# Recurrence gates of a hybrid encoder layer on TensorE: two heads in the two row halves, both gates in the columns

## The chip, the cores and the metric

The kernel runs on one core of one Trainium2 chip. The metric is the device time of one execution in microseconds (us); lower is better. The engines are TensorE (PE, whose weight loads are listed apart as PEld), VectorE (DVE), ScalarE (ACT), GpSimd (POOL) and SyncE (SP), which here only asks for transfers. A line number such as L821 is a line of the kernel before.

## The reference, cut to what matters

One layer on 512 tokens of width 1024: a half-step SwiGLU FFN, a mixer with two branches (a gated linear recurrence, and sliding-window attention), and a second half-step FFN. The change is in the recurrence's gates, which are block-diagonal: 16 heads of 64 channels, each with its own 64x64 matrix for each of two gates.

```python
def rg_lru(x, wa, ba, wx, bx, lam):
    xb = xf.reshape(b, s, LRU_BLOCKS, LRU_BLOCK)          # 16 heads of 64 channels
    r = jax.nn.sigmoid(jnp.einsum('bshi,hij->bshj', xb, wa).reshape(b, s, LRU_WIDTH) + ba)
    ig = jax.nn.sigmoid(jnp.einsum('bshi,hij->bshj', xb, wx).reshape(b, s, LRU_WIDTH) + bx)
    log_a = -LRU_C * r * jax.nn.softplus(-lam)
    a = jnp.exp(log_a)
    u = jnp.sqrt(-jnp.expm1(2.0 * log_a)) * (ig * xf)
    # then the scan h[t] = a[t] * h[t-1] + u[t] over the tokens
```

x here is the input projection's x_rnn after a causal convolution of four taps.

## The kernel before

**Precision.** A float32 product is made of three matmuls in the fp32r format: each operand is split into a high part (ACT copies it) and a rest (DVE subtracts), and high x high, rest x high and high x rest are added up in one PSUM bank. `split2` (L188) splits activations, `split_to` (L148) the weights: L155 on ACT, L156 on DVE.

**Layout.** Activations are kept channels x tokens: a tile is 128 channels by 512 tokens, one PSUM bank (`bank`, 8 of them). A "unit" (`unit`, L206) is one 128-channel tile of a projection: `mm_feat` (L193) makes 24 matmuls of 512 columns (lines L200 to L202). Weights come in 512 KB pieces by transfers that SP asks for in a fixed `order` (L99), as buffers come free. All big tiles come from one pool of 42 buffers (`slot`), in turn.

**Order of work.** PE's order is that of the program text. What ACT, DVE and POOL do beside a unit is put in by `later(n, fn, rank)` (L174): it is due n points later, and `point()` (L178), called twice in a unit, runs what is due. So the order on every engine is fixed when the program is built, and each engine works its own list in order, waiting on semaphores.

**The recurrence.** After the first FFN the eight x_rnn tiles are made (`xr`), then the first eight of the branch gates (`wg`), then k, v, q. Beside them, for each of the eight channel tiles i: `conv`; `rg_gates(i)` (L810) splits the convolved tile into `xs`, and two points later `products` (L818) puts six matmuls of 128 rows x 128 columns x 512 tokens between the units' matmuls, three for each gate, into the banks `r` and `i`. The weight of a gate is a 128x128 block with the two heads' 64x64 matrices on its diagonal and zeros elsewhere; `rg_load` (L780) clears a buffer on POOL, brings the matrices in with two transfers and splits it, once for each gate. One point later `gates` (L825) takes a tanh of each bank on ACT (L826, L827) and one product on DVE (L828); a sigmoid is made from the tanh of half its argument, so the biases are halved once in `softplus` (L704). `rg_decay` and `rg_scan` follow.

**The start.** Nine matmuls on zeros (L602) warm PE. Then ACT's list has a table load with a one-column square root (L607) and the request for the first 128 rows of x transposed (`load_x(0, act)`, L608); SP asks for the vector of small parameters (`vec`, L609), for the weights of the first three units in quarters (`load_w`) and for the other rows of x. L642, L643 and L649 to L651 are the split of x and the first units' matmuls.

Of the kernel before, what the change touches and what calls it, by code (L numbers as in the profile page):

```python
# [10 lines left out]
F32 = mybir.dt.float32  # L11
F32R = mybir.dt.float32r
AF = mybir.ActivationFunctionType
ALU = mybir.AluOpType

P = 128
SEQ = 512
D = 1024
KT = D // P
# [12 lines left out]
V_CW, V_CB, V_BA, V_BX, V_LAM, V_BG, V_G1, V_SINK, V_N = 0, 32, 40, 48, 56, 64, 80, 88, 104  # L32
# [19 lines left out]
def hybrid_layer(ctx: ExitStack, tc: tile.TileContext, a: dict, out: bass.AP):  # L52
    nc = tc.nc
    act, dve, pool, pe, sp = nc.scalar, nc.vector, nc.gpsimd, nc.tensor, nc.sync

    cp = ctx.enter_context(tc.tile_pool(name="cp", bufs=1))
# [6 lines left out]
    def slot(shape, dt=F32, name="s"):  # L63
        uid[0] += 1
        return sb.tile(shape, dt, tag="slot", name=f"{name}_{uid[0]}")

    def bank(name="ps"):
        uid[0] += 1
        return pp.tile([P, 512], F32, tag="ps", name=f"{name}_{uid[0]}")

    def small(w, name="m", bufs=4):
        uid[0] += 1
        return sm.tile([P, w], F32, tag=f"sm{w}", name=f"{name}_{uid[0]}", bufs={1: 11, 4: 12}.get(w, bufs))

    def f32(ap):
        return ap.bitcast(F32)
# [3 lines left out]
    vec = cp.tile([P, V_N], F32, name="vec")  # L80
    chalf = cp.tile([P, KT], F32, name="chalf")
    cneg = cp.tile([P, KT], F32, name="cneg")
    bhalf = cp.tile([P, 4 * KT + 8], F32, name="bhalf")

    cp.tile([P, 192], F32, name="gap")
    sm.tile([P, 256], F32, name="gap2", bufs=1)
    uT = cp.tile([P, 2, KT, SEQ], F32R, name="uT")

# [71 lines left out]
    def get(nm, i, ahead=2, rawahead=3):  # L160

        k = st["get"]
        assert order[k] == (nm, i), (order[k], nm, i)
        dma_to(k + 1 + ahead)
        split_to(k + 1 + ahead)
        dma_to(st["split"] + rawahead)
        st["get"] += 1
        return pairs.pop(k)
# [5 lines left out]
    def later(n, fn, rank=1):  # L174
        uid[0] += 1
        due.append((now[0] + n, rank, uid[0], fn))
# [11 lines left out]
    def split2(hi, lo, src):  # L188

        act.activation(hi, src, AF.Copy)  # L190
        dve.tensor_tensor(out=lo, in0=src, in1=f32(hi), op=ALU.subtract)  # L191
# [14 lines left out]
    def unit(nm, i, **kw):  # L206
        w = get(nm, i)
        ps = bank("f")
        mm_feat(ps, w, **kw)
        return ps  # L210
# [12 lines left out]
    def rstd_of(ssq, scale=1.0, during=lambda q: None):  # L223

        n = ssq.shape[-1]
        w = 1 if n == 2 else n
        v, q, r, e, r2 = (small(w, x) for x in ("v", "q", "r", "e", "r2"))
        if n == 2:
            dve.tensor_scalar(out=v, in0=ssq[:, 0:1], scalar1=ssq[:, 1:2], scalar2=D * EPS, op0=ALU.add, op1=ALU.add)
        else:  # L230
            dve.tensor_scalar(out=v, in0=ssq, scalar1=D * EPS, scalar2=None, op0=ALU.add)
        act.activation(q, v, AF.Sqrt)
        during(q)
        dve.reciprocal(r, q)
        if w == 1:
            dve.scalar_tensor_tensor(out=e, in0=r, scalar=v, in1=r, op0=ALU.mult, op1=ALU.mult)
        else:
            dve.tensor_tensor(out=e, in0=r, in1=r, op=ALU.mult)
            dve.tensor_tensor(out=e, in0=e, in1=v, op=ALU.mult)
        s = scale * D**0.5  # L240
        dve.tensor_scalar(out=e, in0=e, scalar1=-0.5 * s, scalar2=1.5 * s, op0=ALU.mult, op1=ALU.add)
        dve.tensor_tensor(out=r2, in0=r, in1=e, op=ALU.mult)
        return r2
# [160 lines left out]
    def silu_mul(ps1, ps3, R=None):  # L404

        t = slot([P, 2, SEQ], name="sw")
        if R is None:
            act.activation(t[:, 0, :], ps1, AF.Silu)
            dve.tensor_tensor(out=t[:, 1, :], in0=ps3, in1=t[:, 0, :], op=ALU.mult)
        else:  # L410
            dve.tensor_tensor(out=t[:, 0, :], in0=ps1, in1=R, op=ALU.mult)
            dve.tensor_tensor(out=t[:, 1, :], in0=ps3, in1=R, op=ALU.mult)
            act.activation(t[:, 0, :], t[:, 0, :], AF.Silu)
            dve.tensor_tensor(out=t[:, 1, :], in0=t[:, 1, :], in1=t[:, 0, :], op=ALU.mult)
        return t[:, 1, :]
# [173 lines left out]
    def load_x(k, q=sp):  # L589
        q.dma_start(out=xts[k // 2][:, k % 2, :], in_=a["xT"][k * P : (k + 1) * P, :])  # L590
# [10 lines left out]
    for _ in range(WARM):  # L601
        pe.matmul(psw, warm[:, :P], warm, start=True, stop=True)  # L602


    tiny = small(4, "tiny")
    dve.memset(tiny, 1.0)
    act.activation(tiny, tiny, AF.Sqrt)  # L607
    load_x(0, act)  # L608
    sp.dma_start(out=vec, in_=a["vec"])  # L609
    for kp in range(KT // 2):  # L610
        load_w(0, kp)
# [18 lines left out]
    ps = [bank("f") for _ in range(NS)]  # L630
# [28 lines left out]
    r = rstd_of(s4, during=lambda q: act.activation(tiny, q, AF.Silu))  # L659
# [26 lines left out]
    def softplus():  # L686
# [16 lines left out]
        dve.tensor_scalar(out=cneg, in0=z[3], scalar1=-4.0, scalar2=None, op0=ALU.mult)  # L703
        dve.tensor_scalar(out=bhalf, in0=vec[:, V_BA : V_BG + 16], scalar1=0.5, scalar2=None, op0=ALU.mult)  # L704

    def swiglu_units(na, nb, f0, f1, hid, R=None):
        for f in range(f0, f1):
            p1, p3 = unit(na, f), unit(nb, f)
            later(1, lambda p1=p1, p3=p3: hid.f.append(silu_mul(p1, p3, R)))
# [45 lines left out]
    for i, at_ in enumerate((end - 5, end - 2, end - 1)):  # L755
        later(at_, lambda i=i: pairs_a.prep(1, i))
    swiglu_units("w1a", "w3a", 2, NC1, hid, Rb)
    point(True)
    X1["b21"] = to_uT(xn[1, 0], 1, 0)
# [17 lines left out]
    hid = None  # L777


    def rg_load(nm):  # L780
        r = slot([P, KT, P], name="rgraw")
        pool.memset(r, 0.0)
        v = a[nm].rearrange("(i two) p q -> two p i q", two=2)
        pool.dma_start(out=r[0:64, :, 0:64], in_=v[0])
        pool.dma_start(out=r[64:128, :, 64:128], in_=v[1])
        hi = slot([P, KT, P], F32R, name="rghi")
        lo = slot([P, KT, P], F32R, name="rglo")
        act.activation(hi, r, AF.Copy)
        dve.tensor_tensor(out=lo, in0=r, in1=f32(hi), op=ALU.subtract)
        return hi, lo  # L790

    rga, rgx = rg_load("rg_a_w"), rg_load("rg_x_w")

    def vcol(base, i):
        return vec[:, base + i : base + i + 1]

    def hcol(base, i):
        return bhalf[:, base - V_BA + i : base - V_BA + i + 1]
# [11 lines left out]
    def rg_gates(i):  # L810
        s0 = lru[i]
        s1 = slot([P, 2, SEQ], name="ig_e")
        lru[i] = (s0, s1)
        xs = slot([P, 2, SEQ], F32R, name="xcs")
        xc, t, ig = s0[:, 0, :], s0[:, 1, :], s1[:, 0, :]
        split2(xs[:, 0, :], xs[:, 1, :], xc)

        def products():  # L818
            pr, pi = bank("r"), bank("i")
            for ps, (wh, wl) in ((pr, rga), (pi, rgx)):  # L820
                pe.matmul(ps, wh[:, i, :], xs[:, 0, :], start=True, stop=False)  # L821
                pe.matmul(ps, wh[:, i, :], xs[:, 1, :], start=False, stop=False)
                pe.matmul(ps, wl[:, i, :], xs[:, 0, :], start=False, stop=True)

            def gates():  # L825
                act.activation(t, pr, AF.Tanh, scale=0.5, bias=hcol(V_BA, i))  # L826
                act.activation(ig, pi, AF.Tanh, scale=0.5, bias=hcol(V_BX, i))  # L827
                dve.scalar_tensor_tensor(out=ig, in0=ig, scalar=1.0, in1=xc, op0=ALU.add, op1=ALU.mult)  # L828

            later(1, gates, 2)  # L830

        later(RG_LAG, products)
# [50 lines left out]
    for i in range(8):  # L883
        ps = unit("wg", i)
# [16 lines left out]
    for i in range(2):  # L901
        ps = unit("wk", i)
# [8 lines left out]
    for t in range(NT):  # L911
        ps = bank("v")
        c = slice(t * P, (t + 1) * P)
        o = ps[:, :256]
        for k in range(KT):
            wh, wl = wv[k // 4]
# [18 lines left out]
    for i in range(2):  # L935
        ps = unit("wq", i)
# [12 lines left out]
    for i in range(8):  # L949
        ps = unit("xg", i)  # L950
# [121 lines left out]
    for nm, i in att_units:  # L1072
        if nm == "lru":
            w = get(nm, i) if i else w_lru
            ps = bank("f")
# [5 lines left out]
        ps = unit(nm, i)  # L1081
# [4 lines left out]
    w = get("wao", 0)  # L1086
# [14 lines left out]
    for i in range(8):  # L1101
        if i:
            w = get("wao", i)
        ps = bank("f")
# [18 lines left out]
    for i, at_ in enumerate((end - 7, end - 4, end - 3, end - 2, end - 1)):  # L1123
        later(at_, lambda i=i: pairs_b.prep(0, i))
    later(end, lambda: pairs_b.prep(1, 0))
    swiglu_units("w1b", "w3b", 2, NC2, hid)
    point(True)
    X2["t4"] = to_uT(tn[3], 0, 1)
# [75 lines left out]
```

## Time and profile before

| | |
|---|---|
| time, median of 3 runs | 1140.14 us (1140.09 to 1140.4) |
| the profiled execution's own time | 1140.29 us |
| its span, first to last instruction | 1138.5 us |
| granted TensorE clock, mean | 0.999 |
| PE, DVE, ACT, POOL busy | 1129.9, 778.5, 572.0, 341.8 us |
| gate matmuls (bank r and bank i) | 48, first 405.8 us, last 460.0 us |

All times of the profile count from the start of the span. A matmul's listed duration is longer than the time from one start to the next, since matmuls are pipelined; so matmuls are priced by the distance of their starts. "Idle before" gives how long the engine sat idle ahead of an instruction, and what released it.

### The profile page before, as it was taken

The numbers are of one execution on the slowest core, as the hardware profiler recorded it, in microseconds if no ns is written. First come the engines' busy times: TensorE is split into PE (matmuls) and PEld (weight loads), VectorE is DVE, ScalarE is ACT, GpSimd is POOL, SyncE is SP. The second block draws the span as 40 slices with busy tenths as digits, with TensorE's granted clock in tenths as the row PEclk, the third lists the DMA queues.
The fourth block names the chain that finished last, engine by engine and source line by source line (L and its number), as shares of the span: only waits on it lengthen the run. The fifth ranks groups of instructions, "written<-read, shape, count | busy, mean of one in ns | idle before, by whom it ended". The sixth has DMA issues, their size and how long they took to land.

```text
span 1138.5 us, 17073 instructions
## 1 busy us (share of the span) xinstructions
PE 1129.9 (99%) x6691; PEld 1006.8 (88%) x6691; DVE 778.5 (68%) x1180; ACT 572.0 (50%) x1021; POOL 341.8 (30%) x259
## 2 busy tenths in 40 slices
PE   9999999999999999999999999999999999999997
PEld 7889999988889888888888888889899999998886
DVE  5997889885447746684678864667968678985313
ACT  7445555564325357844656662356445555574211
POOL 0148677500001000001555640000655567700000
PEclk9999999999999999999999999999999999999999
DMA  9943323265314311234122333532133332255101
GB/s 339 155 138 112 100 88 111 87 210 166 98 57 152 120 56 56 90 97 130 56 78 90 93 99 105 170 126 93 37 94 112 112 98 89 93 189 180 39 19 55
DMA packets 36800, 124.93 MB, mean 110 GB/s; under 512 B 4400, under 2 KB 5936, under 8 KB 36720
## 3 DMA queue, kind: packets, MB, share of 16 engines
q1 hardware_dynamic: 34128, 115.15, 30.6%
q0 software_dynamic: 2448, 8.43, 3.9%
q8 instruction: 52, 0.85, 0.3%
q10 hardware_dynamic: 144, 0.26, 0.1%
q14 instruction: 28, 0.23, 0.1%
HBM read 116.50 MB, written 7.33 MB: 109 GB/s over the span
## 4 chain that ended last, share of the span: by engine, by line
PE 94%; DMA 4%; DVE 1%; SPq 0%; ACT 0%; issue 0%; DVEq 0%; ACTq 0%
PE f L201 11%; PE f L202 11%; PE f L200 11%; PE c L453 10%; PE c L452 10%; PE c L451 10%; PE acc L219 8%; PE acc L218 8%; PE acc L220 8%; DMA raw_w1a<-in_w1a_dram 2%; PE pt L1019 1%; DMA h<-in_x_dram 1%; PE s L983 1%; PE s L982 1%; PE tr L291 1%; PE o L1035 1%
## 5 line engine op out<-in xcount | busy, mean ns | idle before, releaser
L200 PE MATMUL f<-uT,whi 128*128 128x512 f32 (+1 forms) x536 | 196.1, 366 | 0.0
L201 PE MATMUL f<-uT,wlo 128*128 128x512 f32 (+1 forms) x536 | 195.2, 364 | 0.3 <-DVE wlo L156 0.3
L202 PE MATMUL f<-uT,whi 128*128 128x512 f32 (+1 forms) x536 | 195.1, 364 | 0.0
L218 PE MATMUL acc<-whi,hT 128*128 128x512 f32 x352 | 137.1, 390 | 0.0
L219 PE MATMUL acc<-wlo,hT 128*128 128x512 f32 x352 | 137.0, 389 | 0.0
L220 PE MATMUL acc<-whi,hT 128*128 128x512 f32 x352 | 136.9, 389 | 0.0
L201 PEld LDWEIGHTS f<-uT,wlo 128*128 128x128 f32 x536 | 101.2, 189 | 16.4 <-DVE wlo L156 0.7
L191 DVE TENSOR_TENSOR wlo<-S,whi 128x1024 fp32r<-128x1024 f32 x68 | 112.8, 1659 | 4.1 <-ACT whi L190 3.8
L453 PE MATMUL c<-Xl,whi 128*128 128x256 f32 x408 | 115.5, 283 | 0.0
L453 PE MATMUL c<-uT,whi 128*128 128x256 f32 x408 | 115.5, 283 | 0.0
L452 PE MATMUL c<-Xh,wlo 128*128 128x256 f32 x408 | 115.5, 283 | 0.0
L452 PE MATMUL c<-uT,wlo 128*128 128x256 f32 x408 | 115.5, 283 | 0.0
L451 PE MATMUL c<-Xh,whi 128*128 128x256 f32 x408 | 115.5, 283 | 0.0
L451 PE MATMUL c<-uT,whi 128*128 128x256 f32 x408 | 115.5, 283 | 0.0
L202 PEld LDWEIGHTS f<-uT,whi 128*128 128x128 f32 x536 | 101.1, 189 | 15.9
L200 PEld LDWEIGHTS f<-uT,whi 128*128 128x128 f32 x536 | 101.2, 189 | 15.6
L1003 POOL TENSOR_SCALAR P<-P,d 128x256 f32<-128x256 f32 (+1 forms) x64 | 63.1, 1001 | 56.0 <-DVE d L1001 33.9
L452 PEld LDWEIGHTS c<-Xh,wlo 128*128 128x128 f32 x408 | 78.3, 192 | 0.0
L452 PEld LDWEIGHTS c<-uT,wlo 128*128 128x128 f32 x408 | 78.3, 192 | 0.0
L451 PEld LDWEIGHTS c<-Xh,whi 128*128 128x128 f32 x408 | 78.3, 192 | 0.0
L451 PEld LDWEIGHTS c<-uT,whi 128*128 128x128 f32 x408 | 78.3, 192 | 0.0
L453 PEld LDWEIGHTS c<-uT,whi 128*128 128x128 f32 x408 | 78.3, 192 | 0.0
(313 smaller groups left out, 2673.7 us busy)
## 6 DMA issues: line engine op xcount, KB each, us to landing
raw_w2a<-in_w2a_dram SPq DMA_DIRECT2D x22, 512.0 KB, 4.1
raw_w1b<-in_w1b_dram SPq DMA_DIRECT2D x22, 512.0 KB, 3.9
raw_w3b<-in_w3b_dram SPq DMA_DIRECT2D x22, 512.0 KB, 3.9
raw_w2b<-in_w2b_dram SPq DMA_DIRECT2D x22, 512.0 KB, 4.2
raw_w3a<-in_w3a_dram SPq DMA_DIRECT2D x21, 512.0 KB, 4.4
raw_w1a<-in_w1a_dram SPq DMA_DIRECT2D x20, 512.0 KB, 4.3
raw_wg<-in_wg_dram SPq DMA_DIRECT2D x16, 512.0 KB, 4.0
raw_xr<-in_xr_dram SPq DMA_DIRECT2D x8, 512.0 KB, 3.9
```

What stands on the lines that cost most here:

```text
L191: dve.tensor_tensor(out=lo, in0=src, in1=f32(hi), op=ALU.subtract)
L200: pe.matmul(ps[:, c0:c1], wh[:, s], h_, start=k == 0, stop=False)
L201: pe.matmul(ps[:, c0:c1], wl[:, s], h_, start=False, stop=False)
L202: pe.matmul(ps[:, c0:c1], wh[:, s], l_, start=False, stop=k == KT - 1)
L218: pe.matmul(acc[n], x[:, 0, c], wh[:, s], start=first, stop=False)
L219: pe.matmul(acc[n], x[:, 0, c], wl[:, s], start=False, stop=False)
L220: pe.matmul(acc[n], x[:, 1, c], wh[:, s], start=False, stop=last)
L291: pe.transpose(ps[:, k * P : (k + 1) * P], hg[:, kk * P : (kk + 1) * P], ident)
L451: pe.matmul(ps, wh[:, s], xh, start=first, stop=False, skip_group_check=True)
L452: pe.matmul(ps, wl[:, s], xh, start=False, stop=False, skip_group_check=True)
L453: pe.matmul(ps, wh[:, s], xl, start=False, stop=k == 3, skip_group_check=True)
L1003: pool.tensor_scalar(out=pt[:, x, b0:256], in0=pt[:, x, b0:256], scalar1=d[:, x : x + 1], scalar2=None, op0=ALU.mult)
```

## The change

A gate's two heads no longer share a 128-row matmul in which half of the weights are zero. One weight tile `rgw` holds both gates: in rows 0 to 63 (the lower head of the channel tile) columns 0 to 63 are the matrix of gate r and columns 64 to 127 that of gate i; in rows 64 to 127 (the upper head) it is the other way round. A matmul takes 64 rows of weights and of activations and gives both gates of one head. There are still six matmuls for a channel tile, now 64 rows x 128 columns x 512 tokens, in turn for rows 0 to 63 (bank `r`) and rows 64 to 127 (bank `i`). The tanh is taken in four pieces of 64 partitions, two of which go to the other half of the partitions, so `bxh` holds the halved bias of gate i in both halves (16 columns, taken off the unused `gap`). `rg_load` runs once, without a clear. Apart from that, the request for the first rows of x comes ahead of the square root on ACT's list.

```diff
-    cp.tile([P, 192], F32, name="gap")
+    bxh = cp.tile([P, 2, KT], F32, name="bxh")
+    cp.tile([P, 176], F32, name="gap")
...
+    load_x(0, act)
     tiny = small(4, "tiny")
     dve.memset(tiny, 1.0)
     act.activation(tiny, tiny, AF.Sqrt)
-    load_x(0, act)
     sp.dma_start(out=vec, in_=a["vec"])
...
         dve.tensor_scalar(out=bhalf, in0=vec[:, V_BA : V_BG + 16], scalar1=0.5, scalar2=None, op0=ALU.mult)
+        for par in range(2):
+            for r0 in (0, 64):
+                dve.tensor_scalar(
+                    out=bxh[r0 : r0 + 64, par, :], in0=vec[64 * par : 64 * par + 64, V_BX : V_BX + KT],
+                    scalar1=0.5, scalar2=None, op0=ALU.mult)
...
-    def rg_load(nm):
+    def rg_load():
         r = slot([P, KT, P], name="rgraw")
-        pool.memset(r, 0.0)
-        v = a[nm].rearrange("(i two) p q -> two p i q", two=2)
-        pool.dma_start(out=r[0:64, :, 0:64], in_=v[0])
-        pool.dma_start(out=r[64:128, :, 64:128], in_=v[1])
+        for nm, cs in (("rg_a_w", (0, 64)), ("rg_x_w", (64, 0))):
+            v = a[nm].rearrange("(i two) p q -> two p i q", two=2)
+            for par, c in enumerate(cs):
+                pool.dma_start(out=r[64 * par : 64 * par + 64, :, c : c + 64], in_=v[par])
...
-    rga, rgx = rg_load("rg_a_w"), rg_load("rg_x_w")
+    rgw = rg_load()
...
         def products():
-            pr, pi = bank("r"), bank("i")
-            for ps, (wh, wl) in ((pr, rga), (pi, rgx)):
-                pe.matmul(ps, wh[:, i, :], xs[:, 0, :], start=True, stop=False)
-                pe.matmul(ps, wh[:, i, :], xs[:, 1, :], start=False, stop=False)
-                pe.matmul(ps, wl[:, i, :], xs[:, 0, :], start=False, stop=True)
+            ps = bank("r"), bank("i")
+            for n, (w, x) in enumerate(((0, 0), (1, 0), (0, 1))):
+                for p_, r_ in zip(ps, (slice(0, 64), slice(64, P))):
+                    pe.matmul(p_, rgw[w][r_, i, :], xs[r_, x, :], start=n == 0, stop=n == 2)
 
             def gates():
-                act.activation(t, pr, AF.Tanh, scale=0.5, bias=hcol(V_BA, i))
-                act.activation(ig, pi, AF.Tanh, scale=0.5, bias=hcol(V_BX, i))
+                lo_, up = slice(0, 64), slice(64, P)
+                for p_, r_ in zip(ps, (lo_, up)):
+                    act.activation(t[r_], p_[r_], AF.Tanh, scale=0.5, bias=hcol(V_BA, i)[r_])
+                for par, (p_, r_, o_) in enumerate(((ps[0], up, lo_), (ps[1], lo_, up))):
+                    act.activation(ig[o_], p_[r_], AF.Tanh, scale=0.5, bias=bxh[r_, par, i : i + 1])
                 dve.scalar_tensor_tensor(out=ig, in0=ig, scalar=1.0, in1=xc, op0=ALU.add, op1=ALU.mult)
```

## The prediction, made before the changed kernel ran

> **What bounds the kernel.** I read the page's busy table first, then PE's waits, the timeline around one set of gate products, and the timelines of ACT beside it and of the start.
>
> ```profile
> PE 1129.9 (99%) x6691; PEld 1006.8 (88%) x6691; DVE 778.5 (68%) x1180; ACT 572.0 (50%) x1021; POOL 341.8 (30%) x259
> ```
>
> ```profile
> PE w L602 <- DVE tiny L606: 1.4, 1, 1.4
> PE f L201 <- DVE wlo L156: 0.3, 1, 0.3
> ```
>
> The first line is the share of the span, the others are all that PE waited for, in us, times and longest. Apart from its first 1.4 us PE stops once, for 0.3 us. So from about 1.5 us to the end the time is the sum of the distances between matmul starts, and what is taken off PE is taken off the end, until another engine or a transfer takes PE's place. The timeline of one channel tile (start, duration):
>
> ```profile
> 405.59 0.39 PE L202 MATMUL f<-uT,whi 128*128 128x512 f32 x1
> 405.81 0.39 PE L821 MATMUL r<-xcs,rghi 128*128 128x512 f32 x1
> ...
> 406.50 0.39 PE L821 MATMUL i<-xcs,rghi 128*128 128x512 f32 x1
> ...
> 407.18 0.39 PE L200 MATMUL f<-uT,whi 128*128 128x512 f32 x1
> ```
>
> Six gate matmuls and two of their neighbours: seven steps from 405.59 to 407.18 are 1.59 us, 0.227 us each. One tile's six cost 6 x 0.227 = 1.36 us, the eight tiles 10.9 us, all on the path.
>
> **The gate products.** The change keeps 48 matmuls of 512 columns, in 24 pairs whose halves use different rows of the array. No row shows two matmuls side by side, so a pair is bounded. Below, one step, 0.227 us. Above, two steps, 0.454 us, if the halves take turns; beyond that only if weight loads stop running ahead (a rival). I take 0.23: a pair also needs two weight loads of 128 columns, and the eight 128-column transposes L291 take 0.87 us, 0.109 us for a load and its matmul, so two loads (0.218 us) fit into a step.
>
> Between 128-row and 64-row matmuls the array changes its shape, once in and once out for a tile. The nearest rows are the only matmul of less than 128 rows (L667, 32 rows), and the restart after PE's only stop:
>
> ```profile
> 27.61 0.39 PE L202 MATMUL f<-uT,whi 128*128 128x512 f32 x1
> ...
> 27.93 0.11 PEld L667 LDWEIGHTS e<-oh 32*16 32x16 f32 x2 [0.35 <-issue]
> ...
> 28.26 0.48 PE L667 MATMUL e<-oh 32*16 32x384 f32 x1
> ...
> 28.67 0.19 PEld L676 LDWEIGHTS r<-dgs,ones 128*128 128x128 f32 x1 [0.64 <-issue]
> 28.67 0.38 PE L676 MATMUL r<-dgs,ones 128*128 128x128 f32 x1
> ...
> 57.56 0.19 PEld L201 LDWEIGHTS f<-uT,wlo 128*128 128x128 f32 x1 [0.70 <-DVE wlo L156]
> 57.56 0.50 PE L201 MATMUL f<-uT,wlo 128*128 128x512 f32 x1 [0.27 <-DVE wlo L156]
> ...
> 57.90 0.40 PE L202 MATMUL f<-uT,whi 128*128 128x512 f32 x1
> ```
>
> Into L667 the distance is 0.32 us instead of 0.227, 0.09 more; its weight load (PEld) begins with the matmul, not ahead of it. Out of it, 28.26 to 28.67 is 0.41 us against 0.33 from its first pass (27.93) to its second, 0.08 more. L667 loads only 16 columns. At 57.56 a 128-column load stood in the open, and the next start came 0.34 us later, 0.11 above a step. So I take 0.11 in and 0.08 out, 0.19 us for a tile. Below nothing it can't go; above, I take each change as waiting out the matmul before it (0.39 listed less the 0.227 step, 0.16) and then an open load (0.11), 0.54 us for the two.
>
> A tile then takes 3 x 0.23 + 0.19 = 0.88 us instead of 1.36, 0.48 saved, 8 x 0.48 = **3.84 us**. The ends are 8 x (0.68 - 0) = 5.4 and 8 x (0.68 - 0.54) = 1.1 us.
>
> The Trainium skill (TensorEngine Tiling, Key Properties) speaks against the change at this point: changing the tiling mode drains TensorE. The 0.09 and 0.08 us above agree that a change costs something, but not with a full wait for the matmul before (0.16).
>
> **The gates on ACT.** Two tanh of 128x512 (0.69 us each) become four of 64x512. Half the partitions are hardly cheaper: copies of 64x512 from PSUM (L892) take 0.59 us. So a tile adds 1.2 to 1.4 us to ACT. One turn of ACT, from one tile's gates to the next:
>
> ```profile
> 446.13 0.69 ACT L826 ACTIVATE xc_t<-r,bhalf 128x512 f32<-128x512 f32 x1 [1.15 <-PE r L823]
> 446.81 0.69 ACT L827 ACTIVATE ig_e<-i,bhalf 128x512 f32<-128x512 f32 x1
> ...
> 449.53 0.69 ACT L881 ACTIVATE g<-f,bhalf 128x512 f32<-128x512 f32 x1 [0.56 <-PE f L202]
> ...
> 450.96 0.82 ACT L840 ACTIVATE xc_t<-xc_t,chalf 128x512 f32<-128x512 f32 x1
> 452.93 0.69 ACT L826 ACTIVATE xc_t<-r,bhalf 128x512 f32<-128x512 f32 x1 [1.15 <-PE r L823]
> ```
>
> The turn is 6.80 us, and ACT idles 0.56 + 1.15 = 1.71 us in it, both times for PE. PE's turn becomes 6.80 - 0.48 = 6.32 us; ACT's work becomes 5.09 + 1.3 = 6.4. ACT is full and slips at most 0.2 us a turn, some 1.2 us over the six turns at this rate. What is late next: the products of DVE (L828) and behind them on its list the weight rests L156, whose wait for ACT grows by two tanh; and the weight copies L155 behind the tanh on ACT. PE takes these weights later: the rests for wq 0 are written by 472.8 us and first used at about 480; the tightest, for xg 2, by 497.86, used at about 502, and DVE is 98% busy from 480 to 500. That run begins behind ACT's square roots at 477.5; ACT idles 1.08 + 0.75 + 0.75 us between 463 and 476, which takes up the slip. Cover: 4 us of lead, of which 1 to 2 go. Cost nothing; if the cover were gone, the slip, 1.2 us. Bank r is now held through the third tanh, 1.3 us longer; a turn takes three of the eight banks, so a bank comes round after 2.7 turns, 17 us.
>
> **The small edits.** The single `rg_load` drops two POOL clears (0.96 us each), one ACT copy (1.06) and one DVE subtraction (1.22); its four transfers stay, on the same POOL queue. PE has no idle time from 360 to 380 us, so nothing is gained. The four `bxh` products of 64x8 go after L704 at 250.5 us, by the 128x8 rows near it 0.2 us each, 0.8 us on DVE, which is 93% busy from 245 to 255; behind them stand the rests of the second FFN matrix. DVE idles 0.73 us at 257 and 2.1 at 261, waiting, and PE never stops there: nothing, or 0.8 if the cover failed. Three buffers fewer shift later tiles in the pool and so the waits of SP's weight transfers; those are asked for far ahead (wk at 383 and 407 us, copied at 441 and 447, 3.6 us to land), so nothing.
>
> **The first rows of x.**
>
> ```profile
> 0.73 0.38 SPq L609 DMA_DIRECT2D vec<-in_vec_dram  x1
> 1.46 0.38 ACTq L590 DMA_DIRECT2D xt<-in_xT_dram  x1
> 3.56 0.42 ACT L190 ACTIVATE whi<-raw_first 128x256 fp32r<-128x256 f32 x1 [1.34 <-DMA raw_first<-in_w1a_dram]
> 4.79 0.72 ACT L642 ACTIVATE uT<-xt,vec 128x512 fp32r<-128x512 f32 x1 [0.81 <-DMA xt<-in_xT_dram]
> 5.57 0.80 PE L649 MATMUL f<-uT,whi 128*128 128x512 f32 x1
> ```
>
> ACT's queue asked for x (L590) at 1.46 us; now nothing stands ahead of the request, and it goes out at about 0.73 like SP's first. The split of x (L642) waited for it until 4.79 and PE's first real matmul for that. The table load moves 0.4 us later, to end at about 2.4, before ACT's copy at 3.56. PE could start up to 0.73 us earlier. But PE's stop at 57.56 is for a rest that DVE wrote, DVE having been 97 to 100% busy since 36 us, and that work begins with the rows of h, landed at 23.45 behind all the first transfers on engines that were full from 2.5 us on (shares 0.90 to 1.14). A gain before the stop lasts only as far as the transfers move too. From 1.5 to 2.5 us the DMA engines were idle 0.5 x 0.70 + 0.5 x 0.40 = 0.55 us, which an earlier request can fill. I take **0.3 us**, with 0 and 0.73 as ends; a loss is excluded, since the split needs both x and the weights and the bytes are the same.
>
> **Sum.** 3.84 + 0.3 = 4.14 us off the profiled execution: 1140.29 - 4.14 = 1136.15 us, a span of about 1134.4. The median stands 0.15 below that execution, so 1136.0.
>
> **The rivals.**
> - Halves take turns: the pair costs 0.454, and only the shape changes are new: + 8 x 0.19 - 0.3 = +1.2, 1141.3 us. For it: no row shows an overlap. Against it: different rows and different banks. The change would then not do what it says.
> - The second half starts only when its own load is through, 0.109 us after the first: a pair takes 0.336, a tile 1.20, saving 0.16 x 8 + 0.3 = 1.6, 1138.5 us. The Trainium skill (TensorE: Matmul & The Clock Gate, Measured speedup vs the span model) has 3.07 of 4 for four row tiles; at that share a pair would take 0.295 us by my estimate and the time be about 1137.5. No run here shows it yet.
> - ACT bounds the turn: its 6.46 us (with 1.37 added) instead of 6.80 save 0.34 a turn over seven turns, 2.4 + 0.3, 1137.4 us. For it: ACT full. Against it: the 4 us of lead.
> - Slower: in the 64-row shape no weight load runs ahead, so every matmul pays the open load seen at 57.56. 48 x 0.11 + 8 x 0.19 - 0.3 = +6.5, 1146.6 us. For it: L667's load began with its matmul (0.35 us of PEld idle before). Against it: that is one load, at a change. It decides from a pair of 0.39 us on, where 3 x 0.39 + 0.19 is the 1.36 of before.
>
> **How the numbers follow.** The forecast has 0.70, turns 0.10, the late second half 0.08, ACT 0.06, open loads 0.06. About 0.2%, 2.3 us, is what a measurement of this kernel can tell from no change: faster is below 1137.9. The forecast's upper end, both changes at 0.54 and no gain at the start, is 1140.14 - 1.1 = 1139.0; I put 0.04 of its 0.70 above 1137.9. Faster 0.66 + 0.05 of ACT's = 0.71; same 0.04 + 0.01 + 0.10 + 0.08 = 0.23; slower 0.06. The lower end is 1140.14 - 5.4 - 0.7 = 1134.0. From 1134.0 to 1139.0 takes in the forecast, ACT and the late half; turns and open loads, 0.16, stay out.
>
> **What the profile after would show.** Right: the two halves of a pair start together, pairs 0.23 us apart, about 0.1 us extra at each shape change; ACT without idle time from 419 to 460 us, its turn near 6.4; PE still with no wait but the one near 57 us; the last gate products about 4 us earlier, and the end by as much. Wrong: starts 0.227 us apart inside a pair, PE waits for L155 or L156 between 410 and 505 us, or an end that moves less than the gates.

## The result, and the profile after

The changed kernel takes **1138.61 us** (median of 22 runs, 1138.19 to 1138.8), the kernel before beside it 1140.28 us (22 runs, 1140.06 to 1140.76): ratio 0.9984, interval 0.9978 to 0.9991. It is faster, by 1.67 us; the forecast was 4.14. The direction held and the time lies in the range, but the size was off by a factor of 2.5. The profiled execution's span went from 1138.5 to 1136.9 us.

The busy table of the page, and all of PE's waits:

```profile
PE 1128.2 (99%) x6691; PEld 1001.0 (88%) x6691; DVE 778.7 (68%) x1183; ACT 582.2 (51%) x1036; POOL 340.7 (30%) x257
```

```profile
PE w L603 <- DVE tiny L608: 1.5, 1, 1.5
PE f L202 <- DVE wlo L157: 0.3, 1, 0.3
```

PE is still the bound, and no wait was added: ACT has 10 us more work, and PE never stops for it. So the missing 2.5 us are not in a wait. They must be in the distances between matmul starts. The timeline of the tile that was shown of before (PE, the weight loads left out but three):

```profile
405.88 0.39 PE L203 MATMUL f<-uT,whi 128*128 128x512 f32 x1
406.20 0.18 PEld L832 LDWEIGHTS r<-xcs,rghi 64*128 64x128 f32 x1 [0.35 <-issue]
406.20 0.49 PE L832 MATMUL r<-xcs,rghi 64*128 64x512 f32 x1
...
406.20 0.49 PE L832 MATMUL i<-xcs,rghi 64*128 64x512 f32 x1
406.31 0.19 PEld L832 LDWEIGHTS r<-xcs,rglo 64*128 64x128 f32 x1
...
406.54 0.39 PE L832 MATMUL r<-xcs,rglo 64*128 64x512 f32 x1
...
406.54 0.39 PE L832 MATMUL i<-xcs,rglo 64*128 64x512 f32 x1
...
406.77 0.39 PE L832 MATMUL r<-xcs,rghi 64*128 64x512 f32 x1
406.77 0.39 PE L832 MATMUL i<-xcs,rghi 64*128 64x512 f32 x1
407.10 0.19 PEld L201 LDWEIGHTS f<-uT,whi 128*128 128x128 f32 x1 [0.37 <-issue]
407.10 0.50 PE L201 MATMUL f<-uT,whi 128*128 128x512 f32 x1
...
407.44 0.40 PE L202 MATMUL f<-uT,wlo 128*128 128x512 f32 x1
```

The starts are 405.88, 406.20, 406.54, 406.77, 407.10, 407.44. The two halves of a pair start together: the overlap is complete. But of five distances only one is a step of 0.23. The others are 0.32, 0.34, 0.33 and 0.34: **each change of shape costs twice**, once before the first matmul in the new shape (+0.09 in, +0.10 out) and once behind it (+0.11 each), because its weight load stands in the open (the PEld rows with "0.35 <-issue" and "0.37 <-issue" begin with their matmuls, not ahead of them, while the load at 406.31, inside the burst, stands 0.23 us ahead of its matmul). What the 0.09 to 0.10 ahead of the first matmul are made of, the trace doesn't show. From 405.88 to 407.44 it is 1.56 us; five steps would be 1.14, so the two changes cost 0.42. Before, eight steps of 0.227 us took 1.82 us there. A tile saves about 0.25 us, not 0.48. Eight tiles give 1.97 us when the starts of the two traces are set against each other one by one.

One turn of ACT, from one tile's gates to the next:

```profile
445.43 0.69 ACT L837 ACTIVATE xc_t<-r,bhalf 64x512 f32<-64x512 f32 x1
446.14 0.69 ACT L837 ACTIVATE xc_t<-i,bhalf 64x512 f32<-64x512 f32 x1
446.85 0.69 ACT L840 ACTIVATE ig_e<-r,bxh 64x512 f32<-64x512 f32 x1
447.55 0.68 ACT L840 ACTIVATE ig_e<-i,bxh 64x512 f32<-64x512 f32 x1
448.26 1.06 ACT L156 ACTIVATE whi<-raw_wk 128x1024 fp32r<-128x1024 f32 x1
...
451.98 0.69 ACT L837 ACTIVATE xc_t<-r,bhalf 64x512 f32<-64x512 f32 x1
...
458.54 0.69 ACT L837 ACTIVATE xc_t<-r,bhalf 64x512 f32<-64x512 f32 x1 [0.54 <-PE r L832]
```

A tanh over half the partitions costs what a full one cost, 0.69 us. ACT has no idle time in its turn of 6.55 us (445.43 to 451.98), which is PE's own (27 x 0.227 + 0.42 = 6.55); before the last tile it waits for PE again.

The start:

```profile
0.73 0.40 ACTq L591 DMA_DIRECT2D xt<-in_xT_dram  x1
...
1.45 4.21 PE L603 MATMUL w<-warm 128*128 128x512 f32 x9 [1.45 <-DVE tiny L608]
...
4.33 0.71 ACT L643 ACTIVATE uT<-xt,vec 128x512 fp32r<-128x512 f32 x1
...
5.46 0.63 PE L650 MATMUL f<-uT,whi 128*128 128x512 f32 x1
```

The request goes out at 0.73 us as intended, and the split of x starts 0.46 us earlier (4.33 after, 4.79 before). The first matmul on data moves by 0.11 us only (5.57 to 5.46): it now stands behind the nine matmuls of the warm-up, of which the last starts at 5.03 and takes a step of 0.43. The 19th matmul on data even comes later, at 10.42 us instead of 10.14; rows_only below shows the same start without the early request.

### The profile page after: what moved, and what is told of

It is laid out like the page before. It is cut to its first block, busy times and chain, and to the rows that moved or that the text cites. A ratio compares the mean times of both kernels' runs of the same rounds, so it can differ in the third digit from the quotient of the medians.

```text
span 1136.9 us, 17091 instructions
## 1 busy us (share of the span) xinstructions
PE 1128.2 (99%) x6691; PEld 1001.0 (88%) x6691; DVE 778.7 (68%) x1183; ACT 582.2 (51%) x1036; POOL 340.7 (30%) x257
## 4 chain that ended last, share of the span: by engine, by line
PE 97%; DVE 2%; ACT 0%; issue 0%; DVEq 0%
PE f L201 11%; PE f L202 11%; PE f L203 11%; PE c L454 10%; PE c L453 10%; PE c L452 10%; PE acc L220 8%; PE acc L221 8%; PE acc L219 8%; PE pt L1032 1%; PE s L996 1%; PE s L995 1%; PE tr L292 1%; PE r L832 1%; PE o L1048 1%; PE o L1049 1%
## 5 line engine op out<-in xcount | busy, mean ns | idle before, releaser
L452 PEld LDWEIGHTS c<-uT,whi 128*128 128x128 f32 x408 | 78.3, 192 | 0.0
L454 PEld LDWEIGHTS c<-Xl,whi 128*128 128x128 f32 x408 | 78.3, 192 | 0.0
```

Of the source, the lines that this page charges most:

```text
L452: pe.matmul(ps, wh[:, s], xh, start=first, stop=False, skip_group_check=True)
L454: pe.matmul(ps, wh[:, s], xl, start=False, stop=k == 3, skip_group_check=True)
```

## The experiments

The theory after this reading: the gates save 1.97 us because a change of shape costs 0.2 us each way, and the request for x saves nothing. The rivals: the gates save the forecast 3.84 and something elsewhere gives it back (ACT, the start); or the halves don't really run together. Beside rows_only, x_only, pairs_apart and two_tiles the kernel before took 1140.38 us, beside warm_7 and warm_7_x_late 1140.36, beside the others 1140.25.

### The two parts of the change, each by itself

rows_only is the changed kernel with the request for x at its old place, x_only the kernel before with the request moved:

```diff
-    load_x(0, act)
     tiny = small(4, "tiny")
     dve.memset(tiny, 1.0)
     act.activation(tiny, tiny, AF.Sqrt)
+    load_x(0, act)
```

> The change to the gates alone; the request for the first rows of x stays where it was. Theory: each tile's six gate matmuls are three overlapped pairs (0.227 us each) plus one change of the array's shape in and out, 0.43 us, so a tile saves 0.25 us and eight save 2.0; the earlier request for x costs 0.3. Then this run is 2.0 us faster than before (1138.3) and 0.3 faster than the changed kernel (1138.6). Rival: the request for x costs nothing and the tiles save only 1.65 in the end, the rest being given back further on: 1138.6.

Measured: 1138.43 us (11 runs, 1138.17 to 1138.84), ratio 0.9983 (0.9975 to 0.9992): 1.95 us less than before.

> The kernel before with only the request for the first rows of x put first. Theory: the warm-up's last matmul ends at 5.45 us, so PE's first real one can gain at most 0.12 us, and the third unit's first weights and the next rows of x land later behind the first rows, so PE falls 0.28 us behind by its 13th matmul and keeps that: 1140.55. Rival 1: no effect, 1140.3. Rival 2, the prediction's: 0.3 us faster, 1140.0.

Measured: 1140.5 us (11 runs, 1140.22 to 1140.81), ratio 1.0001 (0.9992 to 1.001). The gates carry all of the gain. The request alone shows none: the median is 0.12 us above that of the kernel before, though the interval, about 1 us to either side, is too wide to tell the theory's loss of 0.28 from nothing. The traces show that this loss needs no early request. In rows_only, with the request at its old place, the 19th matmul on data starts at 10.45 us, as late as in the changed kernel (10.42); in x_only it starts at 10.10. Over the eight profiles of this document with nine matmuls of warm-up and the early request it lies between 9.78 and 10.52, with the late request at 10.14 (before) and 10.45. So 0.28 us is within what the start varies by, and can't be laid on the early request.

### What a change of shape costs

pairs_apart puts three matmuls of the unit between the pairs, so that a tile changes shape six times instead of twice (the last two lines stand in `mm_feat`, behind a unit's next three matmuls):

```diff
+            def pair(n, w, x):
+                for p_, r_ in zip(ps, (slice(0, 64), slice(64, P))):
+                    pe.matmul(p_, rgw[w][r_, i, :], xs[r_, x, :], start=n == 0, stop=n == 2)
+            pair(0, 0, 0)
+            apart.extend([lambda: pair(1, 1, 0), lambda: pair(2, 0, 1)])
...
+            elif apart:
+                apart.pop(0)()
```

> The changed kernel with the three pairs of a tile set apart by three 128-row matmuls each, so that the array changes its shape three times in and out for a tile. Theory: a shape change in and out costs 0.43 us wherever it stands, so 16 more cost 6.9 us: 1145.5. Rival 1: the 0.43 us belongs to the start of a tile (its operands or banks, once for a tile): no slower than 1139. Rival 2: ScalarE, full through this stage, sets the turn of a tile, and PE's own cost is hidden under it: clearly less than 6.9 us more.

Measured: 1145.54 us (4 runs, 1145.5 to 1145.64), ratio 1.0045 (1.003 to 1.0061), 6.9 us above the changed kernel: 16 x 0.43. The gates are now slower than the 128-row form that they replaced. One excursion on PE's timeline:

```profile
405.62 0.39 PE L205 MATMUL f<-uT,whi 128*128 128x512 f32 x1
...
405.94 0.50 PE L836 MATMUL r<-xcs,rghi 64*128 64x512 f32 x1
...
406.37 0.50 PE L203 MATMUL f<-uT,whi 128*128 128x512 f32 x1
...
406.71 0.39 PE L204 MATMUL f<-uT,wlo 128*128 128x512 f32 x1
```

0.32 + 0.43 + 0.34 = 1.09 us where three steps would be 0.68: 0.41 for one way in and out, as in the changed kernel, with a single pair in the other shape. So neither rival holds: the cost stands at every change, not once for a tile, and ACT hides none of it.

all_rows takes the change of shape away and keeps the three steps: three matmuls over all 128 rows in place of the three pairs. It adds the two heads of a tile into one another, so its gates are not the reference's.

```diff
-            ps = bank("r"), bank("i")
+            ps = (bank("r"),) * 2
...
-                for p_, r_ in zip(ps, (slice(0, 64), slice(64, P))):
-                    pe.matmul(p_, rgw[w][r_, i, :], xs[r_, x, :], start=n == 0, stop=n == 2)
+                pe.matmul(ps[0], rgw[w][:, i, :], xs[:, x, :], start=n == 0, stop=n == 2)
```

> The changed kernel with three matmuls over all 128 rows and 128 columns in place of three pairs over 64 rows (the two heads of a tile are then added into one another, so the gates are not the reference's). The work on PE keeps its three steps and loses the change of shape alone. Theory A, the change of shape costs 0.41 to 0.43 us for a tile, in and out, and nothing else holds the stage: 8 x 0.43 = 3.4 us less than the changed kernel, about 1135.2, and every distance in the stage 0.227. Rival B, ACT, whose turn in the changed kernel is 6.56 us beside PE's 6.55, takes over as the bound: less is gained, from 0 (1138.6) to about 1 us (1137.6), with idle time of PE on a bank that ACT still reads. Rival C, the prediction's price of 0.19 for a tile was right and the missing part is elsewhere: 1.5 us less, 1137.1.

Measured: 1135.37 us (5 runs, 1134.8 to 1135.7), ratio 0.9955 (0.9943 to 0.9968): 3.24 us less than the changed kernel against 3.4 expected of the change of shape at 0.43, and 1.5 at the forecast's price. Every distance around a tile is a plain step again, four of them 0.90 us:

```profile
405.55 0.39 PE L203 MATMUL f<-uT,whi 128*128 128x512 f32 x1
405.77 0.39 PE L831 MATMUL r<-xcs,rghi 128*128 128x512 f32 x1
...
406.45 0.39 PE L201 MATMUL f<-uT,whi 128*128 128x512 f32 x1
```

This run leaves out the second bank, too; but so does one_half below, which keeps the 64 rows and pays 0.41 us a tile all the same. This run also settles what ACT would have done with the forecast's gain:

```profile
427.44 1.07 ACT L156 ACTIVATE whi<-raw_wg 128x1024 fp32r<-128x1024 f32 x1
...
431.06 1.37 ACT L836 ACTIVATE xc_t<-r,bhalf 64x512 f32<-64x512 f32 x2
432.45 1.38 ACT L839 ACTIVATE ig_e<-r,bxh 64x512 f32<-64x512 f32 x2
433.86 1.06 ACT L156 ACTIVATE whi<-raw_wg 128x1024 fp32r<-128x1024 f32 x1
```

ACT's turn is 6.42 us, full, while PE's is 27 x 0.227 = 6.13. ACT falls back by 0.29 us a turn and PE still has no wait for it: the lead covers a slip larger than the forecast's 0.2. So ACT, full as it is, doesn't set the turn of the changed kernel.

### Whether the halves run together, and by what

one_half leaves the matmuls of rows 64 to 127 out (the gates of every second head are not computed); not_in_turn asks for the three matmuls of rows 0 to 63 (bank `r`) and then for the three of rows 64 to 127 (bank `i`). The two expectations call rows 0 to 63 the upper half and rows 64 to 127 the lower half.

```diff
# one_half
-            ps = bank("r"), bank("i")
+            ps = (bank("r"),) * 2
...
-                for p_, r_ in zip(ps, (slice(0, 64), slice(64, P))):
-                    pe.matmul(p_, rgw[w][r_, i, :], xs[r_, x, :], start=n == 0, stop=n == 2)
+                pe.matmul(ps[0], rgw[w][0:64, i, :], xs[0:64, x, :], start=n == 0, stop=n == 2)
# not_in_turn
-            for n, (w, x) in enumerate(((0, 0), (1, 0), (0, 1))):
-                for p_, r_ in zip(ps, (slice(0, 64), slice(64, P))):
+            for p_, r_ in zip(ps, (slice(0, 64), slice(64, P))):
+                for n, (w, x) in enumerate(((0, 0), (1, 0), (0, 1))):
```

> The changed kernel with the lower half's three matmuls left out (both reads go to the upper half's bank, so the gates of every second head are not computed). Theory A, the lower half runs wholly in the shadow of the upper half: no change beside the changed kernel, 1138.6 (1138.2 to 1139.0), and the rows of a tile's matmuls keep their distances, 0.33, 0.34, 0.23 into and 0.33, 0.34 out of the tile. Rival B, the second half costs something of its own (a start apart, a shared feed): up to 0.05 us for each of 24 pairs, 1.2 us, 1137.4.

Measured: 1138.56 us (11 runs, 1137.97 to 1139.11), ratio 0.9983 (0.9975 to 0.9992). The second half costs nothing that can be measured; the distances in and out of the tile are unchanged (0.41 us above five steps, as in the changed kernel).

> The changed kernel with the six matmuls of a tile issued as the upper half's three, then the lower half's three, in place of upper and lower in turn. Theory A, two matmuls run together only where they stand next to each other on PE's list: only the third and the fourth of the six still overlap, five steps of 0.227 us in place of three, +0.45 us for each of eight tiles, 3.6 us, about 1142.2 us; the trace would show the matmuls of one tile 0.23 apart but for one pair. Rival B, the two row halves have lists of their own and the order doesn't matter: as the changed kernel, 1138.6, and the lower half's first matmul starts with the upper half's first.

Measured: 1138.76 us (10 runs, 1138.08 to 1139.1), ratio 0.9986 (0.9977 to 0.9995). Theory A falls. On PE's list the three for bank `r` come first, and the trace has the three for bank `i` beside them all the same:

```profile
406.58 0.49 PE L832 MATMUL r<-xcs,rghi 64*128 64x512 f32 x1
406.59 0.49 PE L832 MATMUL i<-xcs,rghi 64*128 64x512 f32 x1
406.92 0.39 PE L832 MATMUL r<-xcs,rglo 64*128 64x512 f32 x1
406.93 0.39 PE L832 MATMUL i<-xcs,rglo 64*128 64x512 f32 x1
407.15 0.39 PE L832 MATMUL r<-xcs,rghi 64*128 64x512 f32 x1
407.16 0.39 PE L832 MATMUL i<-xcs,rghi 64*128 64x512 f32 x1
```

The first matmul of bank `i`, fourth on the list, starts 0.01 us behind the first. The Trainium skill (TensorEngine Tiling (Array Packing), Key Properties) says that tiles work independently, loads and matmuls of different ones in parallel. The trace agrees, over a distance of three list places.

### Fewer changes of shape

two_tiles puts the pairs of two tiles into one burst, so that the eight tiles change shape eight times instead of sixteen; decays are due later, since gates come later:

```diff
-        def products():
+        def products(n_):
...
-        later(RG_LAG, products)
+        held.append(products)
+        if i % 2:
+            later(RG_LAG, lambda ps_=held[:]: [p(n) for n, p in enumerate(ps_)])
+            held.clear()
...
-            later(1, gates, 2)
+            later(1 + n_, gates, 2)
...
-DECAY_AT = (11, 15, 17, 19, 21, 23, 25, 27)
+DECAY_AT = (15, 17, 19, 21, 23, 25, 27, 28)
```

> The changed kernel with the products of two channel tiles in one burst of six pairs (the even tile's wait for the odd one's; decay steps moved behind them), so four shape changes in and out instead of eight. Theory: 4 x 0.43 = 1.7 us less, 1136.9. Rival: ScalarE's turn of 6.56 us, without idle time in the changed kernel, is what PE's turn of 6.56 follows; then the burst brings nothing, 1138.6, or PE shows waits for ScalarE or VectorE between 440 and 505 us.

Measured: 1137.31 us (7 runs, 1137.0 to 1138.17), ratio 0.9974 (0.9963 to 0.9985), 1.3 us less than the changed kernel. From 405 to 470 us the trace gains the 1.7 us on the changed kernel. Behind that it gives 0.65 back, at weight loads that wait for a rest from DVE:

```profile
487.26 0.19 PEld L202 LDWEIGHTS f<-uT,wlo 128*128 128x128 f32 x1 [0.48 <-DVE wlo L157]
...
498.43 0.19 PEld L202 LDWEIGHTS f<-uT,wlo 128*128 128x128 f32 x1 [0.41 <-DVE wlo L157]
```

PE has no wait of its own there that the list of waits shows; the matmuls behind are late by their loads. DVE's scans come 1.2 us later than in the changed kernel, while PE comes 2 us earlier. two_tiles_early brings the last tile's gates and decay a point forward:

```diff
-            later(1 + n_, gates, 2)
+            later(1 + (n_ if i < 7 else 0), gates, 2)
-DECAY_AT = (15, 17, 19, 21, 23, 25, 27, 28)
+DECAY_AT = (15, 17, 19, 21, 23, 25, 26, 27)
```

> The six pairs of two tiles in one burst as in the run before (1137.31), with the last tile's gates and its decay a point earlier. In that run PE gave back 0.65 us between 486 and 511 us: weight loads of L202 waited 0.48 and 0.41 us for wlo from DVE, whose seven scans came 1.2 us later because the last tile's factors were issued after the raw weights of wq. Theory A, the lost part is this order alone: 0.5 to 0.65 us less than that run, 1136.7 to 1136.8. Rival B, ACT's list is merely rearranged and DVE is as late as before: 1137.3, with the same two waits.

Measured: 1137.61 us (10 runs, 1137.35 to 1138.16), ratio 0.9976 (0.9967 to 0.9986). Theory A falls: the two waits are there as before (0.47 and 0.41 us), with the scans no earlier. ACT runs with little idle time from 452 to 476 us in this version; that its list bounds the scans is argued, not shown. Both versions beat the changed kernel by about 1 us, which is what the traces keep of the stage (1.7 less 0.65); the two profiles differ by the start alone (19th matmul on data at 9.78 and 10.33 us).

### What the start is bound by

warm_7 is the changed kernel with seven matmuls of warm-up instead of nine; warm_7_x_late also puts the request for x back to its old place.

```diff
-WARM = 9
+WARM = 7
```

> The changed kernel with seven matmuls of the warm-up in place of nine; the last two took 5.03 minus 0.43 to 5.45 us in its profile, so the cover that they gave the first rows of x is gone. Theory A, the start is bound by the transfers behind the first rows of x (the run with the x request alone had PE wait 0.36, 0.17 and 0.28 us for them in its first eight matmuls): the first matmul on data comes at about 5.05 instead of 5.45, the 28th where it was before (10.2 to 10.4 us after the span's start, 9.7 to 10.5 in the profiles so far), and the time is that of the changed kernel, 1138.6 within 0.3. Rival B, the warm-up alone took the prediction's gain: 0.3 to 0.4 us less, 1138.2 to 1138.3, and a 28th matmul at 9.9. Rival C, with less warm-up the step of 0.43 us lasts longer before it turns to 0.23: each matmul that is still slow costs 0.2 us, two of them 0.4, 1139.0.

Measured: 1138.71 us (11 runs, 1138.45 to 1139.31), ratio 0.9986 (0.9977 to 0.9995): no change. With the cover gone, the first matmul on data starts at 5.29 us (5.05 was expected: PE waits 0.49 us for the split of x) and the 19th (the 28th of all where the warm-up has nine) at 10.46, as in the changed kernel (10.42). So the warm-up was not what kept the gain away (rival B falls).

```profile
5.29 0.79 PE L650 MATMUL f<-uT,whi 128*128 128x512 f32 x1 [0.49 <-ACT uT L643]
```

> The run before with the first rows of x asked for behind the table load again, as the kernel before has it. Theory A, transfers bind the start whichever rows come first: as the run before within 0.3 us. Rival B, with the warm-up's cover gone the early request shows its worth: this one is slower than the run before by the prediction's 0.3 us or more (first matmul on data at 5.55 beside 5.05: up to 0.5).

Measured: 1139.59 us (11 runs, 1138.07 to 1140.7), ratio 0.9992 (0.9983 to 1.0001). The median hides two groups: four runs at 1138.07 to 1138.29 and seven at 1139.5 to 1140.7. The profiled execution is of the second group (1140.31 us):

```profile
1.45 3.35 PE L603 MATMUL w<-warm 128*128 128x512 f32 x7 [1.45 <-DVE tiny L607]
...
5.41 0.80 PE L650 MATMUL f<-uT,whi 128*128 128x512 f32 x1 [0.60 <-ACT uT L643]
...
8.13 0.63 PE L650 MATMUL f<-uT,whi 128*128 128x512 f32 x1
...
8.56 0.63 PE L651 MATMUL f<-uT,wlo 128*128 128x512 f32 x1
...
8.99 0.63 PE L652 MATMUL f<-uT,whi 128*128 128x512 f32 x1
...
10.27 0.58 PE L652 MATMUL f<-uT,whi 128*128 128x512 f32 x1
10.68 0.40 PE L650 MATMUL f<-uT,whi 128*128 128x512 f32 x1
```

After an idle stretch of 0.60 us PE works on in steps of 0.43 us until 10.3 us, where the changed kernel had steps of 0.23 from 6.2 us on. The place where the step turns from 0.43 to 0.23 differs from profile to profile also with nine matmuls of warm-up: at 5.0 us in x_only, 6.1 in the changed kernel, 7.3 in rows_only, and between 4.5 and 7.3 in all ten. These times are those of the first record of the granted clock that each trace holds, a record of the full clock; it begins at 6.5 us in warm_7 and at 10.7 here, each time where the step turns. Ahead of it there is no record, so a granted clock of 1.00 that a view prints for those microseconds is no measurement.

The Trainium skill (TensorE: Matmul & The Clock Gate, Part 1) describes this: a cold array takes 426.7 ns for 512 columns and speeds up after a busy window of about 3.4 us that runs free of the kernel, so that the place varies from run to run. The step agrees (0.43 us here). The same part of the Trainium skill gives the variation once as 500 ns to either side and once as 6, 11 or 14 slow matmuls of one kernel. The 2.8 us between the ten profiles, some seven steps of 0.43, are more than the first and less than the eight of the second.

Neither theory of this run had this; rival C of warm_7 did, at a smaller price. The second group is what B forecast in direction, but not by its mechanism: the four executions of the first group, with the late request, are as fast as any of the changed kernel, and all below the fastest of warm_7 (1138.45). That the other six of the second group lost their time in the same way as the profiled one is argued from their times. What the early request does here is to cut the idle stretch ahead of the first data from 0.60 to 0.49 us, and no execution of warm_7 took longer than 1139.31 us; whether the 0.11 us decide it was not tried further.

## Why the prediction was right or wrong, point by point

- **PE as the bound**: right. The same two waits stand in the list, and what came off the distances came off the end (1.97 us at the gates; 1.95 in the median of rows_only).
- **A pair at 0.23 us**: right (406.54 to 406.77). one_half shows that the second half is free, and so both rivals on the overlap, halves in turn and the late second half, are out. The late half's 1138.5 us lies nearer to the measured 1138.61 than any other time of the prediction, and that is chance: the time alone would have spoken for a mechanism that the rows rule out. The rival with open loads at every matmul in the 64-row shape is out by the same rows: inside a burst the loads run ahead (406.31 for the matmul at 406.54).
- **The change of shape at 0.19 us for a tile: wrong, and this is the step that failed.** It measures 0.41 to 0.43. The two prices that it went by were both right in themselves: 0.09 and 0.08 at L667, where the runs have 0.09 and 0.10, and 0.11 for an open load at 57.56, where the runs have 0.11. The step took one of them for each change (0.11 in, 0.08 out), when they come one after the other, at each change: 0.09 + 0.11 in, 0.10 + 0.11 out. Only the range's upper end (0.54) had both. 8 x (0.42 - 0.19) is 1.8 of the 2.5 us that are missing. The Trainium skill's rule against the change (TensorEngine Tiling (Array Packing), Key Properties) is that a change of mode drains TensorE. The runs agree that a change costs something, more than the 0.09 and 0.08 us that were read for it; that it is a drain they don't show, since the next matmul starts 0.32 to 0.33 us behind one that is listed with 0.39.
- **ACT**: right that it becomes full, that four tanh of 64 partitions cost twice as much as two of 128 (ACT busy +10.2 us; 8 x 1.3 less the 1.06 of the dropped copy is 9.3), and that PE doesn't wait for it. With PE's turn at 6.55 in place of 6.32 there was no slip to cover; all_rows shows that 0.29 us a turn would have been covered too. The rival with ACT as the bound is out.
- **The small edits at nothing**: right. No wait of PE appeared near them, and the matmuls of the two traces keep their distance of 0.30 us from 60 to 405 us.
- **The first rows of x at 0.3 us: wrong.** The request and the split move as described, but x_only shows no gain. The upper end of 0.73 overlooked the warm-up, whose end at 5.45 leaves 0.12 of it in the changed kernel, and there is nothing behind that cover either: warm_7 gains nothing, and in x_only, where the step turned early, the first matmul on data came 0.34 us earlier (5.23) and the end didn't move. In x_only, whose matmuls were at the short step from the first one on data, the next weight loads wait for the split of x, for ACT's copy and for a weight rest:

```profile
5.79 0.19 PEld L651 LDWEIGHTS f<-uT,whi 128*128 128x128 f32 x1 [0.36 <-DVE uT L643]
6.14 0.19 PEld L649 LDWEIGHTS f<-uT,whi 128*128 128x128 f32 x1 [0.17 <-ACT whi L190]
6.61 0.19 PEld L650 LDWEIGHTS f<-uT,wlo 128*128 128x128 f32 x1 [0.28 <-DVE wlo L191]
```

  Its 19th matmul on data starts at 10.10 us, before the change at 10.14. "A loss is excluded" was not shown wrong: the 0.28 us that the changed kernel's profile loses at the start lie within what moves from one execution to the next, and rows_only loses them without the early request.
- **The sum**: 1.97 at the gates less 0.3 or so at the start is the 1.6 us by which the spans differ. rows_only at 1138.43 and the changed kernel at 1138.61 are not told apart. The median with the early request is 0.1 to 0.2 us above the one without it in two pairs (x_only and before, the changed kernel and rows_only), and warm_7 lies between the two groups of warm_7_x_late; whether it costs something stays open.
- **Range and chances**: the range held at its upper end, which is the one place where the prediction had both prices of a change. By the prediction's own bar (faster below 1137.9) 1138.61 is "the same", which had 0.23, and not "faster", which had 0.71. The bar was coarser than the measurement: the interval excludes no change.

## What to carry to other kernels

A form of matmul that halves the steps but changes the array's shape cost about 0.2 us at each change here (512 columns, 128 rows to 64 and back); so it pays from some two saved steps of 0.227 us a burst on, and the number of bursts counts for more than the number of matmuls in them (pairs_apart lost 6.9 us, two_tiles won 1.3, with the same matmuls). When two rows price two causes that meet at one place, ask whether they exclude each other or come one behind the other before one of them is taken. A gain at the start of a kernel is compared with what moves there from run to run before it is counted.

## What the runs showed of the hardware

- Matmuls on the two row halves start within 0.01 us of each other even when three places apart on PE's list.
- The first weight load behind a change of shape doesn't run ahead, and this costs 0.11 us on top of the 0.09 to 0.10 of the change itself.
- A tanh of 64 partitions takes as long as one of 128 (0.69 us).
- After 0.60 us of idle time at the start the step of 0.43 us lasted to 10.3 us in the profile of warm_7_x_late, whose first gate matmul starts at 407.85 us beside 406.23 in warm_7: 1.6 us of the kernel's time. No execution of warm_7, with 0.49 us of idle time in its profile, took longer than 1139.31 us.
- The step turns from 0.43 to 0.23 us where the trace's first record of the granted clock begins: 5.0 us in x_only, 6.1 in the changed kernel, 7.3 in rows_only, 10.7 in warm_7_x_late. Ahead of that record the views print 1.00 though nothing was recorded, so this slow step has to be read from the distances.
